# Streaming weights in transfers of 1024 columns through four places instead of 2048 columns through two, in a decoder-layer kernel

## The chip, the cores and the metric

The kernel runs on one core of a Trainium2 chip. The metric is the time of one execution on the device in microseconds (us). The core has engines that run their own instruction lists side by side and wait for each other on semaphores: PE (TensorE, the matmuls, with PEld for its weight loads), ACT (ScalarE), DVE (VectorE), POOL (GpSimd) and SP (SyncE, which here only issues transfers). Data come from the device memory by DMA.

## What is computed

One decoder layer on 512 tokens of width 1024, in float32:

```python
f = swiglu(rms_norm(h, ffn1_norm_pre[l]), ffn1_w_gate[l], ffn1_w_up[l], ffn1_w_down[l])
h = h + 0.5 * rms_norm(f, ffn1_norm_post[l])
u = rms_norm(h, mix_norm_pre[l])
proj = u @ w_in[l]
q, k, v, xr, yr, gl = jnp.split(proj, splits, axis=-1)
...
attn_d = attn.astype(x.dtype).reshape(B, S, ATTN_OUT_WIDTH) @ w_attn_branch[l]
...
rec_d = rec @ w_rec_branch[l]
gates = jax.nn.sigmoid(gl).reshape(B, S, N_BRANCHES, D_MODEL)
merged = gates[:, :, 0] * attn_d + gates[:, :, 1] * rec_d
h = h + rms_norm(merged @ w_out[l], mix_norm_post[l])
f = swiglu(rms_norm(h, ffn2_norm_pre[l]), ffn2_w_gate[l], ffn2_w_up[l], ffn2_w_down[l])
h = h + 0.5 * rms_norm(f, ffn2_norm_post[l])
```

with `swiglu(x) = (silu(x @ w_gate) * (x @ w_up)) @ w_down`, a hidden width of 2816, twelve heads of dilated window attention, and a gated linear recurrence (RG-LRU) as the second branch. Nearly all of the data that are read are weights, and each weight is used once.

## The kernel before, in words

**Products.** Each float32 operand is split into a high part and the rest (`split`, L294: ACT copies the high part at L295, then DVE subtracts at L296), and a product is three matmuls: high with high, high with rest, rest with high. Where two matrices are multiplied with the same input, or a product can be cut in four quarters, seven products of half size stand for eight (`seven`, L738; `seven_on`, L709; `seventh`, L699, with the matmuls at L705 to L707). For these, sums of the weights' quarters are needed; `w_forms` (L661) makes them on DVE (L668 to L670 and L673) and then splits four results `a`, `b`, `c` and `d` on ACT and DVE. `w_forms_within` (L681) does the same in another order.

**The two feed-forward parts** (`ffn`, L772) go through 22 hidden blocks of 128. The first few (6 in the first part, 3 in the second) are plain products (`std`). Each later block `f` has one weight block `gu` of 2048 columns (gate and up side by side), whose forms are made one block ahead (`prep`), and one product of seven (`prod`). Hidden blocks come in parts of four; the products with the down matrix of a finished part are put beside the next blocks in four steps (`prepd` with `d_forms`, L883, and `down7`, L947, matmuls at L956 to L958). These steps take 2, 1, 2 and 1 weight blocks of 1024 columns. `merge` (L967) adds up the quarters after the last part. Between the two feed-forward parts stand the mixer's stages: values, queries and keys (double blocks named `pair`), attention, recurrence, output.

**The stream.** All weights lie in device memory in the order of use. `stream_plan` (L103) lists the blocks with their widths; `stream_groups` (L159) packs consecutive blocks into groups of at most `RAW_W` = 2048 columns, and a group is one transfer of up to 1024 KB (128 partitions of 8 KB). `raw_of` (L232) hands out the next block of the list; with the first block of a group it takes a place of the tag `raw` (two places, L238) and issues the transfer on SP (L240). A place can be written again when all readers of what it held are done. A double block (`gu`, `pair`, and `vq`, four of them for the values, two of which go straight to buffers of their own) fills one place. Two blocks of 1024 share one if they follow each other and neither is cut off by a double block. A single block of 1024 between two double blocks has a whole place to itself.

**Order.** The kernel is written as one program, and `tc.high_priority(offset=...)` moves instructions ahead: the fetching and forming of weights by `AHEAD` = 100, the taking of results out of the accumulators by `EVAC` = 200. From the priorities, the dependences and the expected readiness of data, a fixed order of instructions for each engine comes out when the program is built. At run time an engine goes through its list in that order and waits where an operand is not there. SP issues the stream's transfers in the order of use.

**The start.** `fetch_start` (L270) loads eight blocks of 512 columns into two places by eight transfers, each beside a piece of the input.

Of the kernel before, what the change touches and what calls it, by code (L numbers as in the profile page):

```python
# [10 lines left out]
F32 = mybir.dt.float32  # L11
# [5 lines left out]
P = 128  # L17
T = 512
D = 1024
# [9 lines left out]
NH = 4  # L29
EPS = 1e-6  # L30
HB = 256
RAW_W = 2048
NEG = -1.0e30

FIRST_ON = {1: 5, 2: 5}
# [67 lines left out]
def stream_plan():  # L103

    plan = []

    def down(n, a, half):
        for kk in range(part_blocks(a)):
            plan.append((("down", n, a, half, kk), 1024))

    def ffn(n):
        for ev in ffn_order(n):
            if ev[0] == "std":
                plan.append((("gate", n, ev[1]), 1024))
                plan.append((("up", n, ev[1]), 1024))
            elif ev[0] == "prep":
                plan.append((("gu", n, ev[1]), 2048))
            elif ev[0] == "prepd":
                for q in SEVEN_RAW[ev[2]]:
                    plan.append((("dq", n, ev[1], q), 1024))  # L120
        for half in range(2):
            down(n, len(FF_PARTS) - 1, half)

    def qk(h):
        for g in range(NG):
            plan.append((("pair", g * 4 + h, 12 + g * 4 + h), 2048))

    ffn(1)
    del plan[:4]
    for k in range(KC):  # L130
        plan.insert(k, (("start", k), 512))
    for k in range(4):
        plan.append((("v", 0, k), 1024))
    for q in ("g0", "g1", "u0", "u1"):
        plan.append((("vq", q), 2048))
    for h in range(NH):
        qk(h)
    for c in range(0, KC, 2):
        plan.append((("pair", 52 + c, 53 + c), 2048))
    for m in range(0, KC, 2):  # L140
        plan.append((("attn", m), 1024))
    for what, h in LRU_ORDER:
        if what == "gates":
            plan.append((("lru", h), 1024))
        elif (what, h) in PAIRED:
            plan.append((pair_key(what, h), 2048))
        else:
            for c in GATE1[h] if what == "gate1" else (2 * h, 2 * h + 1):
                plan.append((("in", COLUMN[what] + c), 1024))
    for m in range(KC):  # L150
        plan.append((("rec", m), 1024))
    for half in range(2):
        for kk in range(4):
            plan.append((("out", half, kk), 1024))
    ffn(2)
    return plan


def stream_groups():  # L159
# [22 lines left out]
def hybrid_layer(ctx: ExitStack, tc: tile.TileContext, xT: bass.AP, xN: bass.AP, wst: bass.AP,  # L182
                 first: bass.AP, rows: bass.AP, consts: bass.AP, bias: bass.AP, out: bass.AP):
    nc = tc.nc
    DVE, ACT, PE = nc.vector, nc.scalar, nc.tensor
# [3 lines left out]
    wpool = ctx.enter_context(tc.tile_pool(name="wpool", bufs=4))  # L189
# [42 lines left out]
    def raw_of(key, dst=None):  # L232

        g, i = state["g"], state["i"]
        grp = groups[g]
        if i == 0:
            w = grp[-1][1] + grp[-1][2]
            raw = dst if dst is not None else wpool.tile([P, RAW_W], F32, name="raw", tag="raw", bufs=2)  # L238
            src = bass.AP(tensor=wst.tensor, offset=wst.offset + state["off"], ap=[[w, P], [1, w]])
            nc.sync.dma_start(raw[:, :w], src)  # L240
            state["raw"] = raw
            state["off"] += w * P
        k, o, w = grp[i]
        assert k == key, (k, key)
        src = state["raw"][:, o:o + w]
        if i + 1 == len(grp):
            state["g"], state["i"] = g + 1, 0
        else:
            state["i"] = i + 1
        return src  # L250

    def fetch(key, slot=None, ahead=0):

# [15 lines left out]

    def fetch_start():  # L270

        raws = [wpool.tile([P, RAW_W], F32, name="raw", tag="raw", bufs=2) for _ in range(2)]
        wts = []
        for k in range(KC):
            raw = raws[k // 4][:, (k % 4) * 512:(k % 4) * 512 + 512]
            if k == 0:
                raw = first_t[:, :512]
                nc.sync.dma_start(hm(k), xT[k])
                nc.sync.dma_start(raw, first[:, :512])
            else:  # L280
                nc.sync.dma_start(raw, bass.AP(tensor=wst.tensor, offset=wst.offset + (k - 1) * 512 * P,
                                               ap=[[512, P], [1, 512]]))
                nc.sync.dma_start(hm(k), xT[k])
            if k % 2 == 0:
                wt = w8()
            o = (k % 2) * 512
            wts.append((wt[:, 0, o:o + 512], wt[:, 1, o:o + 512], raw))
        state["g"], state["off"] = KC, (KC - 1) * 512 * P
        return wts
# [4 lines left out]
    def split(dh, dl, src):  # L294
        ACT.activation(dh, src, AF.Copy)  # L295
        DVE.tensor_sub(dl, src, dh.bitcast(F32))  # L296
# [364 lines left out]
    def w_forms(key):  # L661

        with tc.high_priority(offset=AHEAD):
            raw = raw_of(key)
            u0, u1, g0, g1 = (raw[:, i * 512:(i + 1) * 512] for i in range(4))
            s12 = spool[0].tile([P, 2, 512], F32, name="s12", tag="s", bufs=2)
            s1, s2 = s12[:, 0, :], s12[:, 1, :]
            DVE.tensor_add(s2, u0, u1)  # L668
            DVE.tensor_add(s1, s2, g0)
            DVE.tensor_add(u0, u0, g0)  # L670
            a, b, c, d = w8(), w8(), w8(), w4()
            split(a[:, 0, :], a[:, 1, :], raw[:, 1024:2048])
            DVE.tensor_add(g1, s1, g1)  # L673
            split(b[:, 0, :], b[:, 1, :], s12.rearrange("p s c -> p (s c)"))
            split(c[:, 0, :], c[:, 1, :], raw[:, 0:1024])
            split(d[:, 0, :], d[:, 1, :], g1)
            lo, hi = slice(0, 512), slice(512, 1024)
            return {"p1": a[:, :, lo], "p2": a[:, :, hi], "p6": b[:, :, lo], "p5": b[:, :, hi],
                    "p7": c[:, :, lo], "p4": c[:, :, hi], "p3": d}

    def w_forms_within(key):  # L681

        with tc.high_priority(offset=AHEAD):
            raw = raw_of(key)
            u0, u1, g0, g1 = (raw[:, i * 512:(i + 1) * 512] for i in range(4))
            lo, hi = slice(0, 512), slice(512, 1024)
            d, a, c, b = w4(), w8(), w8(), w8()
            split(d[:, 0, :], d[:, 1, :], u1)
            split(a[:, 0, :], a[:, 1, :], raw[:, 1024:2048])
            DVE.tensor_add(u1, u0, u1)  # L690
            DVE.tensor_add(u0, u0, g0)
            DVE.tensor_add(g0, u1, g0)
            split(c[:, 0, :], c[:, 1, :], raw[:, 0:1024])
            DVE.tensor_add(g1, g0, g1)
            split(b[:, 0, :], b[:, 1, :], raw[:, 1024:2048])
            return {"p1": a[:, :, lo], "p2": a[:, :, hi], "p7": c[:, :, lo], "p5": c[:, :, hi],
                    "p6": b[:, :, lo], "p3": b[:, :, hi], "p4": d}

# [327 lines left out]
    u1 = act_of(*act_two(ap1))  # L1026
# [10 lines left out]
    for k in range(KC):  # L1037
        wh, wl, raw = wts[k]
# [48 lines left out]
    with ExitStack() as mx:  # L1087
# [38 lines left out]
        def values_two(steps, then):  # L1126


            def v_of(g):
                return apool.tile([P, 4, T], F32, name="vals", tag=f"v{g}")  # L1130

            def flat(v):
                return v.rearrange("p k t -> p (k t)")

            def add(dst, x, y):
                with tc.high_priority(offset=AHEAD):
                    for h in range(2):
                        cs = slice(h * D, h * D + D)
                        DVE.tensor_add(dst[:, cs], x[:, cs], y[:, cs])

            def form(src):
                with tc.high_priority(offset=AHEAD):
                    ws = [w8(), w8()]
                    for h, w in enumerate(ws):
                        split(w[:, 0, :], w[:, 1, :], src[:, h * D:h * D + D])
                return ws

            def prod(p, w, pss, start):
# [11 lines left out]
                        ACT.activation(dst, ps, AF.Copy, scale=scale)  # L1160

            with tc.high_priority(offset=AHEAD):
                g0, g1 = raw_of(("vq", "g0")), raw_of(("vq", "g1"))
                u0 = raw_of(("vq", "u0"), flat(v_of(1)))
                u1 = raw_of(("vq", "u1"), flat(v_of(2)))
            sd = flat(both[:, 4:8, :])
            b, y, z = [aux_ps(), aux_ps()], [acc_ps(), acc_ps()], [aux_ps(), acc_ps()]
            c5, c6 = ([facc[:, i + j, :] for j in range(2)] for i in (0, 2))
# [192 lines left out]
        for c in range(0, KC, 2):  # L1361
            g, u = tmp("g"), tmp("u")
# [12 lines left out]
    with ExitStack() as mx:  # L1375
# [20 lines left out]
        o, w = SMALL["ap"]  # L1396
# [210 lines left out]
    grow5, _ = gains(ap2, 4)  # L1607
# [58 lines left out]

def _block(key, a):
    kind = key[0]
    if kind in ("gate", "up"):
        return _cols(a[f"ffn{key[1]}_w_{kind}"], key[2] * P)  # L1670
    if kind in ("down", "out"):
        if kind == "out":
            w, r0, half = a["w_out"], key[2] * 2 * P, key[1]
        else:
            w, r0, half = a[f"ffn{key[1]}_w_down"], (FF_PARTS[key[2]][0] + key[4] * 2) * P, key[3]
# [18 lines left out]
    if kind == "start":  # L1694
        k = key[1]
# [47 lines left out]
```

## Time and profile before

| what | value |
|---|---|
| median of 3 runs | 1215.67 us (1215.48 to 1216.31) |
| the profiled execution | 1217.76 us |
| its span, first to last instruction | 1215.9 us |
| what lies around the span | 1217.76 - 1215.9 = 1.9 us |
| mean granted TensorE clock | 0.998 of full |
| read from device memory | 138.06 MB, 119 GB/s with what is written |
| transfers issued on SP at L240 | 107 of 1024 KB and 18 of 512 KB, and 2 of 1024 KB to `vals` |

The profile is that of one execution. Busy time of PE is the union of its matmuls as the profiler models them; matmuls overlap, so a matmul of 128x256 that is recorded with 0.28 us follows the one before it at 0.12 us when nothing holds it up. The chain of waits goes back from the last instruction to what released each one, and in it every matmul has only the time to the next. The table of waits lists, for each engine, how long it stood idle and what ended that; a wait in the middle of an engine's list holds all that is behind it.

### The profile page before, as it was taken

How to read it: one execution, taken by the hardware profiler on the slowest of the kernel's cores; microseconds unless marked ns; L12 is line 12 of the kernel's file. 1: busy time of each engine (PE TensorE's matmuls, PEld its weight loads, DVE VectorE, ACT ScalarE, POOL GpSimd, SP SyncE). 2: the span in 40 equal slices, each digit the busy share in tenths (PEclk: the TensorE clock that was granted, in tenths of full speed). 3: DMA queues.
4: the chain of work that ended last, by engine and by line, in shares of the span. 5: the costliest groups of instructions: out<-in, count | busy, mean ns of one | idle time of the engine just before them, and what ended most of it. 6: DMA issues, size and time to landing. Idle time of an engine off the chain costs nothing.

```text
span 1215.9 us, 19433 instructions
## 1 busy us (share of the span) xinstructions
PE 1204.9 (99%) x7754; PEld 1100.9 (91%) x7754; DVE 1011.2 (83%) x1536; ACT 813.1 (67%) x1391; POOL 26.2 (2%) x51
## 2 busy tenths in 40 slices
PE   9999999999999999999999999999999999999998
PEld 8889999989888999999989888888899999999996
DVE  7999888889689887888766899875798888889964
ACT  7567777777656664665736888934566677878763
POOL 0000000000002000000000000000100000000000
PEclk9999999999999999999999999999999999999999
DMA  6223333334535122222222342224443333333341
GB/s 248 104 87 122 122 121 122 122 121 156 224 126 178 70 81 103 79 82 101 76 99 87 139 160 83 105 104 173 149 148 121 122 122 121 122 122 121 139 174 70
DMA packets 30123, 149.80 MB, mean 123 GB/s; under 512 B 3408, under 2 KB 6864, under 8 KB 16080
## 3 DMA queue, kind: packets, MB, share of 16 engines
q1 hardware_dynamic: 22464, 131.08, 30.2%
q0 software_dynamic: 7280, 17.30, 4.2%
q8 instruction: 61, 1.00, 0.3%
q14 instruction: 30, 0.25, 0.1%
q10 hardware_dynamic: 288, 0.17, 0.0%
HBM read 138.06 MB, written 6.29 MB: 119 GB/s over the span
## 4 chain that ended last, share of the span: by engine, by line
PE 94%; DVE 3%; ACT 2%; DMA 1%; issue 1%; DVEq 0%; ACTq 0%
PE acc L705 15%; PE acc L706 15%; PE acc L707 15%; PE acc L308 7%; PE acc L310 7%; PE acc L309 7%; PE aux L956 4%; PE aux L957 4%; PE aux L958 4%; PE acc L426 2%; PE acc L424 2%; PE acc L425 2%; PE aux L425 1%; PE aux L424 1%; PE aux L426 1%; ACT w L295 1%
## 5 line engine op out<-in xcount | busy, mean ns | idle before, releaser
L705 PE MATMUL acc<-big,w 128*128 128x256 f32 x1240 | 352.0, 284 | 1.9 <-ACT acc L719 1.9
L706 PE MATMUL acc<-big,w 128*128 128x256 f32 x1240 | 351.9, 284 | 0.0
L707 PE MATMUL acc<-big,w 128*128 128x256 f32 x1240 | 351.6, 284 | 0.0
L296 DVE TENSOR_TENSOR w<-raw,w 128x1024 fp32r<-128x1024 f32 (+1 forms) x272 | 297.4, 1099 | 64.7 <-ACT w L295 59.5
L295 ACT ACTIVATE w<-raw 128x1024 fp32r<-128x1024 f32 (+1 forms) x272 | 259.4, 959 | 101.7 <-PE acc L310 39.4
L705 PEld LDWEIGHTS acc<-big,w 128*128 128x128 f32 x1240 | 237.7, 192 | 4.2 <-ACT acc L719 2.1
L706 PEld LDWEIGHTS acc<-big,w 128*128 128x128 f32 x1240 | 237.8, 192 | 1.9
L707 PEld LDWEIGHTS acc<-big,w 128*128 128x128 f32 x1240 | 237.8, 192 | 0.0
L956 PE MATMUL aux<-w,xf 128*128 128x512 f32 x224 | 87.6, 396 | 1.0 <-ACT w L295 1.0
L957 PE MATMUL aux<-w,xf 128*128 128x512 f32 x224 | 88.0, 393 | 0.0
L958 PE MATMUL aux<-w,xf 128*128 128x512 f32 x224 | 87.7, 392 | 0.0
L295 ACT ACTIVATE w<-s 128x1024 fp32r<-128x1024 f32 x51 | 54.0, 1060 | 21.1 <-PE acc L707 13.6
L296 DVE TENSOR_TENSOR w<-s,w 128x1024 fp32r<-128x1024 f32 x51 | 62.2, 1219 | 1.0 <-ACT w L295 0.9
L668 DVE TENSOR_TENSOR s<-raw 128x512 f32<-128x512 f32 x51 | 35.1, 688 | 29.0 <-DMA raw<-in_w 29.0
L308 PE MATMUL acc<-xf,w 128*128 128x512 f32 (+1 forms) x168 | 59.0, 353 | 0.0
L309 PE MATMUL acc<-xf,w 128*128 128x512 f32 (+1 forms) x168 | 58.7, 350 | 0.0
L310 PE MATMUL acc<-xf,w 128*128 128x512 f32 (+1 forms) x168 | 58.5, 349 | 0.0
L719 ACT ACTIVATE c<-acc 128x256 f32<-128x256 f32 x74 | 28.3, 383 | 36.0 <-PE acc L707 35.8
L956 PEld LDWEIGHTS aux<-w,xf 128*128 128x128 f32 x224 | 42.1, 190 | 9.8 <-ACT w L295 2.0
L958 PEld LDWEIGHTS aux<-w,xf 128*128 128x128 f32 x224 | 42.4, 189 | 8.9
L308 PE MATMUL acc<-big,w 128*128 128x512 f32 x128 | 49.8, 389 | 0.0
L309 PE MATMUL acc<-big,w 128*128 128x512 f32 x128 | 49.8, 389 | 0.0
(436 smaller groups left out, 2757.9 us busy)
## 6 DMA issues: line engine op xcount, KB each, us to landing
raw<-in_w SPq DMA_DIRECT2D x107, 1024.0 KB, 4.8
raw<-in_w SPq DMA_DIRECT2D x18, 512.0 KB, 3.5
big<-xf POOLq DMA_DIRECT2D x6, 512.0 KB, 3.3
gains<-in_rows POOLq DMA_DIRECT2D x5, 512.0 KB, 4.2
h<-in_x SPq DMA_DIRECT2D x8, 256.0 KB, 5.2
h<-in_xn POOLq DMA_DIRECT2D x4, 512.0 KB, 6.9
kept_m<-h POOLq DMA_DIRECT2D x4, 512.0 KB, 2.9
vals<-in_w SPq DMA_DIRECT2D x2, 1024.0 KB, 7.0
```

The source lines that it names most:

```text
L295: ACT.activation(dh, src, AF.Copy)
L296: DVE.tensor_sub(dl, src, dh.bitcast(F32))
L308: PE.matmul(ps, wh, xh, start=first, stop=False)
L309: PE.matmul(ps, wh, xl, start=False, stop=False)
L310: PE.matmul(ps, wl, xh, start=False, stop=last)
L424: PE.matmul(ps, x.hi[k][:, bl], wh, start=k == 0 and not seeded, stop=False, skip_group_check=True)
L705: PE.matmul(ps, wh, xh, start=start and k == 0, stop=False, skip_group_check=True)
L706: PE.matmul(ps, wh, xl, start=False, stop=False, skip_group_check=True)
L707: PE.matmul(ps, wl, xh, start=False, stop=k == 3, skip_group_check=True)
L956: PE.matmul(ps, xh, wh, start=first and j == 0, stop=False, skip_group_check=True)
L957: PE.matmul(ps, xh, wl, start=False, stop=False, skip_group_check=True)
L958: PE.matmul(ps, xl, wh, start=False, stop=j == 1, skip_group_check=True)
```

## The change

`RAW_W` goes from 2048 to 1024, and the tag `raw` has four places of 1024 columns instead of two of 2048, in the same memory. `stream_plan` turns every block of 2048 columns into two of 1024 with the keys `lo` and `hi`, so that no group has more than one block of 1024 columns and every transfer of the stream has 512 KB. `raw_two` takes the two halves; `w_forms`, `w_forms_within` and `values_two` take their quarters from two tiles instead of one. The sums and splits are the same in number and size.

```diff
-RAW_W = 2048
+RAW_W = 1024
...
-    return plan
+
+    return [(key + (i,), RAW_W) if width > RAW_W else (key, width)
+            for key, width in plan for i in (("lo", "hi") if width > RAW_W else ("",))]
...
-            raw = dst if dst is not None else wpool.tile([P, RAW_W], F32, name="raw", tag="raw", bufs=2)
+            raw = dst if dst is not None else wpool.tile([P, RAW_W], F32, name="raw", tag="raw", bufs=4)
...
+    def raw_two(key, dst=None):
+
+        return [raw_of(key + (n,), None if dst is None else dst[:, i * RAW_W:(i + 1) * RAW_W])
+                for i, n in enumerate(("lo", "hi"))]
+
...
-        raws = [wpool.tile([P, RAW_W], F32, name="raw", tag="raw", bufs=2) for _ in range(2)]
+        raws = [wpool.tile([P, RAW_W], F32, name="raw", tag="raw", bufs=4) for _ in range(4)]
...
-            raw = raws[k // 4][:, (k % 4) * 512:(k % 4) * 512 + 512]
+            raw = raws[k // 2][:, (k % 2) * 512:(k % 2) * 512 + 512]
...
     def w_forms(key):
 
         with tc.high_priority(offset=AHEAD):
-            raw = raw_of(key)
-            u0, u1, g0, g1 = (raw[:, i * 512:(i + 1) * 512] for i in range(4))
+            ur, gr = raw_two(key)
+            u0, u1, g0, g1 = (r[:, i * 512:(i + 1) * 512] for r in (ur, gr) for i in range(2))
...
             a, b, c, d = w8(), w8(), w8(), w4()
-            split(a[:, 0, :], a[:, 1, :], raw[:, 1024:2048])
+            split(a[:, 0, :], a[:, 1, :], gr)
             DVE.tensor_add(g1, s1, g1)
             split(b[:, 0, :], b[:, 1, :], s12.rearrange("p s c -> p (s c)"))
-            split(c[:, 0, :], c[:, 1, :], raw[:, 0:1024])
+            split(c[:, 0, :], c[:, 1, :], ur)
             split(d[:, 0, :], d[:, 1, :], g1)
...
             with tc.high_priority(offset=AHEAD):
-                g0, g1 = raw_of(("vq", "g0")), raw_of(("vq", "g1"))
-                u0 = raw_of(("vq", "u0"), flat(v_of(1)))
-                u1 = raw_of(("vq", "u1"), flat(v_of(2)))
+                g0, g1 = raw_two(("vq", "g0")), raw_two(("vq", "g1"))
+                u0, u1 = flat(v_of(1)), flat(v_of(2))
+                for q, u in (("u0", u0), ("u1", u1)):
+                    raw_two(("vq", q), u)
```

More of the change, by code (lines that the diff above doesn't have):

```diff
@@ L683, in w_forms_within @@
         with tc.high_priority(offset=AHEAD):
-            raw = raw_of(key)
-            u0, u1, g0, g1 = (raw[:, i * 512:(i + 1) * 512] for i in range(4))
+            ur, gr = raw_two(key)
+            u0, u1, g0, g1 = (r[:, i * 512:(i + 1) * 512] for r in (ur, gr) for i in range(2))
             lo, hi = slice(0, 512), slice(512, 1024)
@@ L688, in w_forms_within @@
             split(d[:, 0, :], d[:, 1, :], u1)
-            split(a[:, 0, :], a[:, 1, :], raw[:, 1024:2048])
+            split(a[:, 0, :], a[:, 1, :], gr)
             DVE.tensor_add(u1, u0, u1)
@@ L692, in w_forms_within @@
             DVE.tensor_add(g0, u1, g0)
-            split(c[:, 0, :], c[:, 1, :], raw[:, 0:1024])
+            split(c[:, 0, :], c[:, 1, :], ur)
             DVE.tensor_add(g1, g0, g1)
-            split(b[:, 0, :], b[:, 1, :], raw[:, 1024:2048])
+            split(b[:, 0, :], b[:, 1, :], gr)
             return {"p1": a[:, :, lo], "p2": a[:, :, hi], "p7": c[:, :, lo], "p5": c[:, :, hi],
@@ L1133, in flat, with two_of @@
                 return v.rearrange("p k t -> p (k t)")
+            def two_of(a):
+                return a if isinstance(a, list) else (a[:, :D], a[:, D:])
             def add(dst, x, y):
                 with tc.high_priority(offset=AHEAD):
-                    for h in range(2):
-                        cs = slice(h * D, h * D + D)
-                        DVE.tensor_add(dst[:, cs], x[:, cs], y[:, cs])
+                    for d, x_, y_ in zip(*(two_of(a) for a in (dst, x, y))):
+                        DVE.tensor_add(d, x_, y_)
             def form(src):
@@ L1143, in form @@
                     ws = [w8(), w8()]
-                    for h, w in enumerate(ws):
-                        split(w[:, 0, :], w[:, 1, :], src[:, h * D:h * D + D])
+                    for w, half in zip(ws, two_of(src)):
+                        split(w[:, 0, :], w[:, 1, :], half)
                 return ws
@@ L1668, in _block @@
     kind = key[0]
+    if key[-1] in ("lo", "hi"):
+        i = ("lo", "hi").index(key[-1])
+        return _block(key[:-1], a).reshape(P, 2, RAW_W)[:, i]
     if kind in ("gate", "up"):
```

## The prediction, made before the result was known

> **What bounds the kernel now.** I begin with the page's busy times, then take what PE itself waited for.
>
> ```profile
> PE 1204.9 (99%) x7754; PEld 1100.9 (91%) x7754; DVE 1011.2 (83%) x1536; ACT 813.1 (67%) x1391; POOL 26.2 (2%) x51
> ```
>
> ```profile
> PE acc L705 <- ACT acc L719: 1.9, 1, 1.9
> PE aux L1033 <- DVE eps L226: 1.1, 1, 1.1
> PE aux L956 <- ACT w L295: 1.0, 5, 0.2
> PE aux L1154 <- DVE w L296: 0.3, 1, 0.3
> ```
>
> PE is busy for 99% of the span, so the change can win only where PE stands still or runs slowly, and these rows (engine, what it waited for, total us, times, longest) are nearly all of that. One wait of 1.9 us is the largest. The wait at L1033 is the program's start, which the change leaves alone. So I look for the 1.9 us in time, by busy time in three stretches of 16 us.
>
> ```profile
> 242.00:258.00 16.00, 16.00 (x114) 15.04 (x113) 14.29 (x20) 13.60 (x24) 0.00 (x0) 1.00 0.30 98
> 258.00:274.00 16.00, 14.13 (x93) 13.09 (x93) 11.23 (x15) 9.51 (x17) 0.00 (x0) 0.89 0.39 132
> 274.00:290.00 16.00, 16.00 (x114) 15.02 (x113) 14.74 (x20) 12.41 (x22) 0.00 (x0) 1.00 0.26 99
> ```
>
> The columns are PE, PEld, DVE, ACT and POOL busy, the granted clock and two of DMA. In the middle stretch PE is busy 14.13 of 16.00 us, and the clock is 0.89 where its neighbours have 1.00. The chain of waits there says why.
>
> ```profile
> 257.78 1.15 DVE w L296
> 258.95 7.32 DMA raw<-in_w
> 266.35 1.06 ACT w L295
> 267.40 0.27 ACT g L877
> 267.68 0.28 ACT acc L719
> 268.00 0.38 PE acc L705
> ...
> 270.04 0.43 PE aux L956
> ```
>
> DVE finished the last split of the double block of hidden block 18, that freed the place, and the transfer of block 19 started and took 7.32 us. ACT stood before the split of its gate half (L295). Behind that in ACT's list were the SiLU of block 18 (L877) and the copy out of an accumulator (L719), which need nothing from that transfer, and PE needs the copy. ACT's timeline has the length of the block:
>
> ```profile
> 266.35 1.06 ACT L295 ACTIVATE w<-raw 128x1024 fp32r<-128x1024 f32 x1 [3.16 <-DMA raw<-in_w]
> ```
>
> The same transfer is usually faster, by the page's list of transfers and that of the stretch before:
>
> ```profile
> raw<-in_w SPq DMA_DIRECT2D x107, 1024.0 KB, 4.8
> raw<-in_w SPq DMA_DIRECT2D x18, 512.0 KB, 3.5
> ```
>
> ```profile
> raw<-in_w SPq DMA_DIRECT2D x1, 1024.0 KB, 7.3
> ```
>
> (The second fence is the answer for 258.5 to 260 us.) So block 19 came 7.3 - 4.8 = 2.5 us late. Elsewhere the forms wait for data too, on DVE (L668) and on ACT (L295), without PE losing:
>
> ```profile
> DVE s L668 <- DMA raw<-in_w: 29.0, 21, 3.1
> ACT w L295 <- DMA raw<-in_w: 13.4, 16, 3.5
> ```
>
> The change therefore acts on a chain (place free, transfer, forms) that is close behind PE in the feed-forward parts, and in one place ahead of it.
>
> **The change part by part.** *More transfers.* 59 double blocks become 118 transfers and the 50 remaining pairs of single blocks become 100; with the 18 single ones that is 236 instead of 127, 109 more. SP issues them:
>
> ```profile
> L240 SPq DMA_DIRECT2D raw<-in_w x125: 327/328/331, 11.3 to 1174.2; - x125
> ```
>
> 109 x 0.33 = 36 us more on SP, whose list holds nothing else but a few loads and the output, and which mostly waits for places to come free (the row of its waits):
>
> ```profile
> SPq L240 <- DVE w L296: 731.8, 96, 22.4
> ```
>
> I cost it at nothing: 36 us lie within 731.8 us of waiting. If both halves start together, the second starts 0.33 us later, which the transfer of the first covers, as it needs 3.5 us. DVE and ACT get one wait more for each double block and no work.
>
> *A half lands earlier.* From 512 KB to 1024 KB the time goes from 3.5 to 4.8 us: 1.3 us for 512 KB, and 2.2 us that don't depend on the size. If a second transfer paid these 2.2 us after the first, the second half would land at 7.0 us. If the 2.2 us overlap, it lands at 4.8 us plus at most 0.33. The nearest rows are those of the next transfer, the second for the stretch of 260.5 to 261.5 us:
>
> ```profile
> 260.93 0.33 SPq L240 DMA_DIRECT2D raw<-in_w  x1
> ```
>
> ```profile
> raw<-in_w SPq DMA_DIRECT2D x1, 1024.0 KB, 7.8
> ```
>
> It landed at 260.93 + 7.8 = 268.7, the one before at 258.95 + 7.3 = 266.3: 2.4 us apart for a whole 1024 KB, less than its 2 x 1.3 of data time. The fixed part overlaps, so I take 4.8 to 5.1 us for both halves. [...]
>
> *Places come free in halves.* The columns of a double block are read last at different times. For block 18, `d` (from the second half) and `c` (from the first) end as follows, and the down blocks of the step before (L899 reads both, the split at 245.09 only `g0`) like this:
>
> ```profile
> 237.37 1.22 DVE L899 TENSOR_TENSOR sum<-raw 128x1024 f32<-128x1024 f32 x1
> ...
> 245.09 1.23 DVE L296 TENSOR_TENSOR w<-raw,w 128x1024 fp32r<-128x1024 f32 x1 [0.51 <-ACT w L295]
> ...
> 255.29 0.69 DVE L296 TENSOR_TENSOR w<-raw,w 128x512 fp32r<-128x512 f32 x1
> ...
> 257.70 1.22 DVE L296 TENSOR_TENSOR w<-raw,w 128x1024 fp32r<-128x1024 f32 x1
> ```
>
> The four places go round: 18 lo, 18 hi, then `u1` of the down blocks in the place of `g0` (free at 246.3), then 19 lo in the place of `u0`, free since 238.6. So 19 lo starts right behind `u1`, near 246.7 instead of 258.95. 19 hi needs the place of 18 lo and starts at 258.95 as before, with half the bytes. Two of every four hidden blocks are like this (after a step with a single down block); in the other two both halves start together and only the first lands earlier. All forms but the first sum need the second half, so what counts is 1.3 us on half of the blocks.
>
> *What that is worth at 258.* If 19 hi is as much slowed as the whole was, it lands 1.3 us earlier, at 265.0; if it takes the usual 3.5 us, at 262.45, before ACT, which became free at 266.35 - 3.16 = 263.19, asks for it. PE loses 16.00 - 14.13 = 1.87 us there now; with 1.3 us of it saved 0.57 remain, with all, nothing. Take 1.6. The clock costs as much again: at 0.89 over 14.13 us of work it is 0.11 x 14.13 = 1.55 us, and the row at 270.04 has 0.43 us for a matmul that elsewhere has 0.24 (below). This fell behind an idle time of 1.87 us; behind the short waits at L956 it didn't. So it goes with the stall, and I take the 1.55 whole. [...]
>
> *The other waits.* The five at L956 look like this one:
>
> ```profile
> 223.03 0.12 PE acc L707
> 223.15 0.23 PE aux L956
> ...
> 225.67 0.24 PE aux L958
> 225.91 0.02 issue
> 225.94 0.60 ACT ea L961
> 226.54 0.95 ACT w L295
> 227.49 0.04 issue
> 227.53 0.73 PE aux L956 x2
> ```
>
> ACT copies an accumulator (L961) and only then splits the weight that PE wants next; no transfer is in the chain. From 225.91 PE has 12 matmuls of the next product at 0.12 us (the row at 223.03), to 227.35; it begins L956 at 227.53 and needs 0.73 us for two matmuls of 0.23: 0.18 + 0.27 = 0.45 us lost. The order of ACT's list decides, so I take no gain, with bounds of plus and minus 5 x 0.45 = 2.3 us.
>
> *Start, values, tail.* In the start the first stream transfer waits behind the start's own on SP; the wait at L1154 ends on DVE work, not on data; the last transfer lands long before the end. Nothing for each.
>
> *Sum.* 1.6 + 1.55 = 3.15 us, say 3.2. The profiled execution has 1217.76 us (1215.9 of span and 1.9 around it): 1217.76 - 3.2 = 1214.6. The runs' median of 1215.67 is 2.1 us below that execution; taken off, **1212.5 us** (-0.26%).
>
> **The rivals.** *(a) No change.* Only here does PE lose to a late transfer, and the 2.1 us between profile and median is near what the stall costs. If the timed runs don't have it, there is nothing to win: 1215.67 less a few tenths, 1215.4. It also comes so if the change doesn't do what it says: where the last split of the first half sets the start, no transfer moves. For it: SP waits mostly for DVE's splits. Against: the list of waits has 21 + 16 = 37 waits for data.
>
> *(b) Slower, by ACT's order.* The order of the lists is made anew from an earlier readiness of data. If forms are put further ahead, ACT stands before a half that isn't there while accumulators wait behind it, which is the chain of 258 in small. The price is that of the small stalls, 0.45 us, in those of the 35 `gu` blocks (16 and 19) whose halves start together, about 18: 8.1 us; -3.2 + 8.1 = +4.9, 1220.6. It decides from 3.2 / 0.45, 7 such blocks, on. For it: DVE and ACT already wait for data 37 times, so the lists are made with data in mind that come too late. Against: no half comes later than its whole did.
>
> *(c) Slower, by the fixed part.* If the 2.2 us are paid one after another, the second half comes 2.2 us later than now. At 258 ACT's 3.16 us cost PE 1.87, so 1.29 are covered; 0.9 us x 35 = 32 us less 3.2: 1244. [...]
>
> *(d) Faster still.* The lists come out better and the five small stalls go too: 1212.5 - 2.3 = 1210.2.
>
> **How the numbers follow.** The forecast with (d) has 0.42 (0.34 and 0.08), (a) 0.27, (b) 0.27, (c) 0.04. A measurement of this kernel can tell about 0.2% from no change, which is 2.4 us; the forecast lies only just beyond. Faster by more than that is the forecast and (d), the same is (a), slower (b) and (c). The range goes from 1209.8, under (d), to 1223, which holds the middle of (b) and leaves out (c) and the worse part of (b).
>
> **What would show it.** Right: the list of transfers has 232 `raw` of 512 KB near 3.5 us; the transfer of 19 lo is issued near 247; the stretch 258 to 274 has PE at 16.00 and a clock of 1.00; L705 no longer waits for L719. Rival (a): the same, but the time stays. (b): more waits of PE on ACT, and longer waits of ACT's L295 for `raw`. (c): transfers of 512 KB with landings near 5.7 us where two start together. It is wrong altogether if the order of ACT or DVE at L295, L719 and L961 differs so much that stalls turn up in stages which have none now.

## The result and the profile after

Over 22 runs of each kernel the median went from 1216.43 us (1213.97 to 1220.45) to 1218.91 us (1216.41 to 1222.43). The ratio is **1.0022, with a 95% interval of 1.0013 to 1.0031: slower by 0.22%**, where 0.26% faster was forecast. The profiled execution of the changed kernel has 1216.87 us and a span of 1215.1 us. It is 2.0 us below its own median, and the profiled one of before lay 1.3 us above its median, so the two spans, 1215.9 and 1215.1, must not be subtracted. The places in the traces count, and the time comes from the runs.

The line numbers move by 7: the split is now L302 (ACT) and L303 (DVE), the matmuls of the sevens L712 to L714, the copy out of an accumulator L726, those of `down7` L963 to L965, and a stream transfer is issued at L242.

The page of the changed kernel, busy times and the stream's transfers:

```profile
PE 1202.6 (99%) x7754; PEld 1099.5 (90%) x7754; DVE 1009.6 (83%) x1536; ACT 816.2 (67%) x1393; POOL 26.1 (2%) x51
...
raw<-in_w SPq DMA_DIRECT2D x232, 512.0 KB, 3.5
```

The transfers are as forecast. The stretch of block 19, in the same columns as before:

```profile
258.00:274.00 16.00, 16.00 (x115) 15.04 (x114) 12.66 (x17) 12.45 (x23) 0.00 (x0) 1.00 0.40 134
```

PE is busy throughout and the clock is 1.00: the stall that the change was forecast to remove is gone. But the list of PE's waits (total us, times, longest) looks like this:

```profile
PE acc L712 <- ACT acc L726: 2.6, 1, 2.6
PE aux L315 <- ACT w L302: 1.5, 1, 1.5
PE aux L1040 <- DVE eps L228: 1.1, 1, 1.1
PE aux L963 <- ACT w L302: 0.7, 3, 0.3
```

The first row has the same pair of lines as the 1.9 us of before, and it is another stall. The chain of waits shows where it is:

```profile
302.56 6.88 DMA raw<-in_w
...
309.47 1.06 ACT act L302
310.52 0.28 ACT acc L726
...
310.85 0.39 PE acc L712
```

It stands at 310 us, at the end of the first feed-forward part. A half with a block of the down matrix took 6.88 us instead of 3.5, ACT stood before its split (into the slot `act`), and the copy that PE needed was behind that in ACT's list. ACT's timeline has the rows:

```profile
306.39 0.37 ACT L884 ACTIVATE g<-acc 128x256 f32<-128x256 f32 x1
309.47 1.06 ACT L302 ACTIVATE act<-raw 128x1024 fp32r<-128x1024 f32 x1 [2.71 <-DMA raw<-in_w]
310.43 0.37 ACT L726 ACTIVATE acc<-acc 128x256 f32<-128x256 f32 x1
```

The second row of the waits is at 690 us, in the recurrence, and has no transfer in its chain:

```profile
686.98 0.60 DVE gt L1538
687.59 0.67 DVE sig L1466
...
688.28 0.02 ACT rec L302
688.31 0.51 issue
688.82 1.05 ACT w L302
...
689.91 0.73 PE aux L315 x2
```

DVE had other work of the recurrence (L1538) ahead of the last sum of `sig` (L1466), ACT waited for that sum with the split of `rec`, and the weight that PE needed was split only after it.

Both are questions of order. Instruction by instruction, the two kernels have the same work on PE, ACT and DVE, but when the program is built other lists come out: 347 of ACT's 1273 places hold another instruction than before, 899 of DVE's 1536, and 758 of PE's 7626 (by the lists as they are written out for the runs below; the page counts some more records of ACT and PE). That gives the theory that I tested: **the transfers and places win what was forecast, and the new order of the lists loses more, most of it at these two places.** The rivals are that the transfers themselves cost time, and that the order costs a little everywhere.

### The profile page after: what moved, and what is told of

Read it like the earlier page. It is cut to its first block, busy times and chain, and to the rows that moved or that the text cites. A ratio compares the mean times of both kernels' runs of the same rounds, so it can differ in the third digit from the quotient of the medians.

```text
span 1215.1 us, 19769 instructions
## 1 busy us (share of the span) xinstructions
PE 1202.6 (99%) x7754; PEld 1099.5 (90%) x7754; DVE 1009.6 (83%) x1536; ACT 816.2 (67%) x1393; POOL 26.1 (2%) x51
## 4 chain that ended last, share of the span: by engine, by line
PE 94%; DVE 2%; ACT 1%; DMA 1%; issue 0%; DVEq 0%; ACTq 0%
PE acc L712 14%; PE acc L713 14%; PE acc L714 14%; PE acc L315 7%; PE acc L317 7%; PE acc L316 7%; PE aux L963 4%; PE aux L964 4%; PE aux L965 4%; PE acc L432 2%; PE acc L431 2%; PE acc L433 2%; DMA raw<-in_w 1%; PE aux L433 1%; PE aux L431 1%; PE aux L432 1%
## 5 line engine op out<-in xcount | busy, mean ns | idle before, releaser
L712 PE MATMUL acc<-big,w 128*128 128x256 f32 x1240 | 351.7, 284 | 2.6 <-ACT acc L726 2.6
L714 PE MATMUL acc<-big,w 128*128 128x256 f32 x1240 | 351.8, 284 | 0.0
L303 DVE TENSOR_TENSOR w<-raw,w 128x1024 fp32r<-128x1024 f32 (+1 forms) x272 | 297.7, 1098 | 45.4 <-ACT w L302 39.7
L302 ACT ACTIVATE w<-raw 128x1024 fp32r<-128x1024 f32 (+1 forms) x272 | 259.7, 958 | 99.1 <-PE acc L317 45.1
L712 PEld LDWEIGHTS acc<-big,w 128*128 128x128 f32 x1240 | 237.6, 192 | 4.7 <-ACT acc L726 2.8
L714 PEld LDWEIGHTS acc<-big,w 128*128 128x128 f32 x1240 | 237.7, 192 | 0.0
L963 PE MATMUL aux<-w,xf 128*128 128x512 f32 x224 | 87.3, 392 | 0.7 <-ACT w L302 0.7
L965 PE MATMUL aux<-w,xf 128*128 128x512 f32 x224 | 87.2, 389 | 0.0
L303 DVE TENSOR_TENSOR w<-s,w 128x1024 fp32r<-128x1024 f32 x51 | 62.2, 1219 | 3.7 <-ACT w L302 3.5
L302 ACT ACTIVATE w<-s 128x1024 fp32r<-128x1024 f32 x51 | 54.0, 1058 | 12.7 <-PE acc L714 9.2
L726 ACT ACTIVATE c<-acc 128x256 f32<-128x256 f32 x74 | 28.2, 382 | 40.7 <-PE acc L714 40.6
L963 PEld LDWEIGHTS aux<-w,xf 128*128 128x128 f32 x224 | 41.9, 188 | 9.1 <-ACT w L302 1.3
L965 PEld LDWEIGHTS aux<-w,xf 128*128 128x128 f32 x224 | 42.1, 188 | 8.8
L315 PE MATMUL acc<-big,w 128*128 128x512 f32 x128 | 49.8, 389 | 0.0
L316 PE MATMUL acc<-big,w 128*128 128x512 f32 x128 | 49.8, 389 | 0.0
L317 PE MATMUL acc<-big,w 128*128 128x512 f32 x128 | 49.8, 389 | 0.0
```

What stands on the lines that cost most here:

```text
L315: PE.matmul(ps, wh, xh, start=first, stop=False)
L316: PE.matmul(ps, wh, xl, start=False, stop=False)
L317: PE.matmul(ps, wl, xh, start=False, stop=last)
L712: PE.matmul(ps, wh, xh, start=start and k == 0, stop=False, skip_group_check=True)
L714: PE.matmul(ps, wl, xh, start=False, stop=k == 3, skip_group_check=True)
L963: PE.matmul(ps, xh, wh, start=first and j == 0, stop=False, skip_group_check=True)
```

## The experiments

All ratios are to the kernel before, run on the same chip alongside, with 95% intervals. e1 and e2 ran on one chip, e3 to e6 on a second, e7 and e8 on a third, so a difference within one of these sets is surer than one between two of them.

| run | what it is | median us | ratio |
|---|---|---|---|
| the change | | 1218.91 | 1.0022 [1.0013, 1.0031] |
| e1 | the change, before's lists | 1213.54 | 0.9980 [0.9971, 0.9989] |
| e2 | before's places and lists, halves as transfers | 1215.21 | 0.9995 [0.9986, 1.0005] |
| e3 | the change, its own lists written out | 1219.27 | 1.0026 [1.0016, 1.0035] |
| e4 | e3, before's order at 294 to 316 us | 1214.89 | 0.9996 [0.9987, 1.0005] |
| e5 | e4, before's order at 641 to 725 us too | 1213.87 | 0.9983 [0.9974, 0.9992] |
| e6 | e1, the change's order at 294 to 316 us | 1220.77 | 1.0041 [1.0028, 1.0053] |
| e7 | e3, the loads of `h` at 301 us cut to 1/8 (the residual of the other columns is left out) | 1215.93 | 1.0004 [0.9994, 1.0014] |
| e8 | the change's order to 294 us, before's from there | 1212.09 | 0.9971 [0.9962, 0.9980] |

**The transfers without the new order (e1).** The order of the three lists is written out and kept by dependences that need no semaphore:

```diff
         hybrid_layer(tc, *args)
+        keep_order(tc)
...
+def keep_order(tc):
+    want = json.loads(zlib.decompress(base64.b85decode(ORDER)))
...
+        for a, b in zip(want[e], want[e][1:]):
+            tc.add_manual_dep(ins[b], ins[a].name, mybir.DependencyInfo(
+                mybir.DependencyClass.NoSync, mybir.DependencyReason.DATA), reason="order")
```

> The changed kernel (four places of 1024 columns, 236 transfers), with the instructions of PE, ACT and DVE held in the exact order that they have in the kernel before. Theory A (order: the 2.5 us come from the new order of the lists, the transfers themselves win a little): ratio to before 0.998 to 1.000, so 0 to 2.5 us faster than before. Theory B (transfers: twice as many transfers are late more often, or cost their waits on DVE and ACT; the order does not matter): ratio near 1.002, 2.5 us slower, as the changed kernel.

The ratio is 0.9980: faster by 0.2%, 2.4 us, beside the 3.2 us of the forecast. PE's wait for L726 isn't in the list of waits any more:

```profile
PE aux L1040 <- DVE eps L228: 1.1, 1, 1.1
PE aux L963 <- ACT w L302: 1.0, 5, 0.2
PE aux L1163 <- DVE w L303: 0.3, 1, 0.3
```

The order alone makes 1.0022 / 0.9980 = 1.0042, or 5.1 us.

**Twice the transfers without the places (e2).** Before's two places of 2048 columns and before's lists, but each transfer of 1024 KB issued as two:

```diff
-            src = bass.AP(tensor=wst.tensor, offset=wst.offset + state["off"], ap=[[w, P], [1, w]])
-            nc.sync.dma_start(raw[:, :w], src)
+            h = min(w, 1024)
+            for o in range(0, w, h):
+                src = bass.AP(tensor=wst.tensor, offset=wst.offset + state["off"] + o * P, ap=[[h, P], [1, h]])
+                nc.sync.dma_start(raw[:, o:o + h], src)
```

> The kernel before with its two places of 2048 columns and its order of instructions held, but each 1024 KB transfer issued as two of 512 KB, one behind the other, into the same place. Only the number and size of the transfers changes. Theory A: ratio 0.999 to 1.001. Theory B: ratio near 1.002. If the first experiment is faster than before and this one is not, what wins is that places come free in halves.

The ratio is 0.9995, with 1 in its interval. Twice the transfers, together with what they save at block 19, cost nothing that can be measured; the further 0.0015 of e1, on the same chip, point to the four places. What is left of block 19's stall is in its waits, 0.5 us (at L707 here) where the kernel before had 1.9:

```profile
PE acc L707 <- ACT acc L721: 0.5, 1, 0.5
```

**Both kernels once more.** One profile more of each, unchanged, to see whether the stalls belong to the kernels:

> The kernel before once more, for a second profile. Both theories: PE loses only little in most places; if the stall of block 19 near 258 us is a rare event, it is not there this time and the span is near 1213 us; if it is fixed, PE again waits 1.9 us for the copy behind the split of block 19.

> The changed kernel once more, for a second profile, since its first profiled execution (1216.87 us) lies 2 us under its median. Theory A: waits of PE on ACT or DVE that stand at the same places as in the first profile (near 310 and 690 us), 2 us or more together. Theory B: PE loses at other places than in the first profile, each time behind a transfer that needs over 5 us.

They do: before again loses PE time at 267 us (16.00 - 14.29 = 1.7 us), and the changed kernel stands until 310.9 and 691.5 us, within 2 us of the places of the first profile. The clock is another matter, below.

**The order written out as it is (e3).** A control: if writing an order out were what gained, this would gain too.

> The kernel after the change with the order of its PE, ACT and DVE lists written out as it has it anyway: a control for the writing out. If the order of the lists is what costs (theory), nothing changes: ratio to the kernel before 1.0022 as measured, within 1.001 and 1.003, with the stalls of 2.7 us at 310 us and 1.7 us at 690 us in place. If the gain of the run with before's order came from writing an order out as such (rival), this run has the gain too: ratio 0.998.

The ratio is 1.0026, so it isn't.

**One place undone (e4).** The lists are those of e3 but for 22 places of ACT's and 17 of DVE's, which hold the same instructions in both orders; in short (`order` stands for a kernel's written-out lists):

```diff
-want = order(after)
+want = order(after); want[ACT][356:378] = order(before)[ACT][356:378]
+want[DVE][359:376] = order(before)[DVE][359:376]
```

> The kernel after the change in its own order, but 22 places of ACT's list and 17 of DVE's (294 to 316 us) in the order of before. Theory (the cost sits in two places, here and at 690 us): the stall of 2.7 to 3.05 us at 310 us goes, 0.23%, and the ratio to before falls from 1.0022 to 0.9998; the stall at 690 us stays. If the clock lost behind the stall (1.8 us more in one of two profiles) goes too, 0.9985. Rival (the cost is spread over the hundred places where the lists differ): the stall goes from the profile but the ratio stays at 1.0015 or above. The transfers at 302 to 308 us should still take near 7 us in either case, since they share the time with the loads of POOL.

The ratio falls from 1.0026 to 0.9996, by 0.0030 or 3.6 us; 0.0024 was forecast for the stall alone and 0.0037 with the clock. The wait at 690 us stays (1.7 us). The half still takes 7.0 us, by the answer for its issue, so what has gone is what stood behind it:

```profile
raw<-in_w SPq DMA_DIRECT2D x1, 512.0 KB, 7.0
```

ACT's timeline of e1, which has the same order here, shows how: the copy comes first, and the splits of the two late blocks stand behind it.

```profile
308.92 0.37 ACT L726 ACTIVATE acc<-acc 128x256 f32<-128x256 f32 x1
...
314.42 1.06 ACT L302 ACTIVATE tx<-raw 128x1024 fp32r<-128x1024 f32 x1 [1.38 <-DMA raw<-in_w]
315.39 1.04 ACT L302 ACTIVATE act<-raw 128x1024 fp32r<-128x1024 f32 x1
```

**The second place undone as well (e5).** The edit is that of e4, with 71 places of ACT's list, 77 of DVE's and 239 of PE's between 641 and 725 us:

> As the run before it, and the stretch of 641 to 725 us also in the order of before on PE, ACT and DVE. Theory: the stall of 1.66 us at 690 us goes as well, 0.14% less than the run with 300 us alone: ratio 0.9985, within 0.1% of the 0.998 with all of before's order; what is left are the three short waits of the last feed-forward part, 0.7 us or 0.06%. Rival (spread): 1.001 or above. If undoing 690 only lets a stall turn up elsewhere, as high as the run with 300 us alone.

The ratio falls by another 0.0013 (1.6 us) to 0.9983, within 0.0003 of e1. The intervals of e4 and e5 overlap, so the second place's share is less sure than the first's. In the chain of waits the split of the weight now stands ahead of that of `rec`, right behind the matmul that frees its place:

```profile
684.68 0.24 PE acc L317
...
684.95 1.06 ACT w L302
686.01 0.53 ACT rec L302
```

So two stretches of the lists, 106 us together, hold 0.9983 to 1.0026 = 0.43% of the 0.46% between e1 and e3. A third place is left in: the last of PE's waits at L963, near 1080 us, is 0.2 us with before's lists, 0.3 us in the changed kernel and 1.4 us in this profile.

**The first place alone (e6).** The reverse of e4: e1 with the change's order at 294 to 316 us.

> The reverse: before's order everywhere (ratio 0.998 so far), with after's order only in the 22 places of ACT's list and 17 of DVE's at 294 to 316 us. Theory: the stall of PE on an accumulator's copy at 310 us is back with 2.6 to 3.1 us, and the ratio is 0.998 + 0.0023 = 1.0003, more by up to 0.0015 if the clock falls behind it. Rival (spread): 0.998 to 0.9985. If the stall needs the earlier order too (when the transfers before it were issued), no stall here and 0.998.

The ratio is 1.0041, 0.0061 (7.4 us) above e1, and more than forecast. Transfer and stall are both larger in this combination (7.63 us, and 3.5 us in the list of waits), and the clock is 0.96 from 300 to 316 us and 0.97 from there to 350. The chain of waits:

```profile
305.69 7.63 DMA raw<-in_w
...
313.34 1.06 ACT act L302
314.40 0.28 ACT acc L726
...
314.72 0.58 PE acc L712
```

In the same stretch a smaller wait appeared that neither order has by itself (L963 waiting for an ACT copy, 1.0 us). The direction is shown; the size is that of this combination.

**The cause of the slow transfer (e7).** At 301 us POOL starts to load `h` for the mixer. The lists are those of e3, but the loads are short:

```diff
     for b in range(4):
-        nc.gpsimd.dma_start(hb(b), xN[b])
+        nc.gpsimd.memset(hb(b)[:, 128:], 0.0)
+        nc.gpsimd.dma_start(hb(b)[:, :128], xN[b][:, :128])
```

> The kernel after the change with its own order written out, but the four loads of h from in_xn at 301 to 304 us bring 128 of 1024 columns, and POOL sets the other columns to zero (so the residual that is added back is left out for them). Theory (the half that ACT waits for at 310 us is slowed by those loads, which share the 16 DMA engines with it): the transfer issued at 302.6 us takes 3.5 to 4.4 us instead of 6.9, lands before ACT is free at 306.8 us, the stall of 2.7 us goes though no list is changed, and the ratio falls from 1.0026 by 0.0022 to 0.0030, to 0.9996 to 1.0004. Rival (the halves slow one another, four in flight on one queue): the transfer still takes 6 us or more, and the ratio stays at 1.002 to 1.003. The stall at 690 us stays in both.

The ratio falls from 1.0026 to 1.0004, without any change of the lists; 0.9996 to 1.0004 was forecast, and the wait at 690 us stays (2.0 us). The transfers issued beside each other are, in the changed kernel (answer for 302.4 to 302.7 us) and in e7 (302.6 to 303 us):

```profile
h<-in_xn POOLq DMA_DIRECT2D x1, 512.0 KB, 5.4
raw<-in_w SPq DMA_DIRECT2D x1, 512.0 KB, 6.9
```

```profile
raw<-in_w SPq DMA_DIRECT2D x1, 512.0 KB, 3.4
h<-in_xn POOLq DMA_DIRECT2D x1, 64.0 KB, 2.1
```

And ACT, which waited 2.71 us there, goes through without waiting:

```profile
306.79 0.36 ACT L884 ACTIVATE g<-acc 128x256 f32<-128x256 f32 x1
307.05 1.05 ACT L302 ACTIVATE act<-raw 128x1024 fp32r<-128x1024 f32 x1
308.00 0.38 ACT L726 ACTIVATE acc<-acc 128x256 f32<-128x256 f32 x1
```

So the stall at 310 us needs both: the loads that slow the half, and the order in which the copy stands behind it. Taking away either one takes it away.

**The better order of each stretch (e8).** Up to 294 us the change's order has none of the small stalls at L963 (e1 has three there), and from 294 us on before's is better:

> Transfers and places of the change; the lists in after's order up to 294 us, where that order has no small stalls, and in before's order from there on, where it has neither the stall at 310 nor the one at 690 us. Theory (stalls at places make up the difference): the three stalls of about 0.36 us at 89, 167 and 227 us of the run with all of before's order go, 1.3 us less than its 1213.5: 1212.2, ratio 0.9970 (0.998 less 0.0011). Rival (each place of the lists has its own noise, and what is saved early is lost again in the stages behind): as that run, 0.998, or up to 0.999.

The ratio is 0.9971, 1212.09 us: faster than both kernels, by 0.3% and 0.5%, with the same transfers and the same work. It is 1.1 us under e1 by the two ratios, but their intervals overlap and the chips differ, so the gain over e1 isn't shown by the times. Its waits for ACT at L963 are down from five to two:

```profile
PE aux L1040 <- DVE eps L228: 1.1, 1, 1.1
PE aux L963 <- ACT w L302: 0.4, 2, 0.2
PE aux L1163 <- DVE w L303: 0.3, 1, 0.3
```

## Why the prediction was wrong

**More transfers: right.** 232 halves of 512 KB with 3.5 us stand in the page, and with the places and lists of before, twice the transfers give 0.9995.

**A half lands earlier, and the fixed parts overlap: right.** In the changed kernel, the two transfers issued together at 235.19 us, the second 0.60 us after the first, took 3.4 and 4.0 us, so both were there 4.6 us after the first was issued; 4.8 to 5.1 was forecast. In e1, the two issued at 286.38 us, again 0.60 us apart, took a median of 4.1 us. The 2.2 us that don't depend on the size are the prediction's estimate from the 3.5 and 4.8 us of before's page; paid one after another, they would have made it 7.0 us.

**Places come free in halves: right for the first half, wrong for the second.** With before's lists, by which the prediction reckons, 19 lo is issued at 246.37 us (e1), and 246.7 was forecast. 19 hi was to need the place of 18 lo and to start at 258.95. It is issued at 256.04, right when the split of `d` ends (255.32 + 0.69 = 256.01), and `d` is read from 18 hi. DVE's and SP's timelines of e1:

```profile
255.32 0.69 DVE L303 TENSOR_TENSOR w<-raw,w 128x512 fp32r<-128x512 f32 x1
```

```profile
256.04 0.33 SPq L242 DMA_DIRECT2D raw<-in_w  x1
```

In the changed kernel, with its own lists, both halves go out earlier still:

```profile
244.55 0.33 SPq L242 DMA_DIRECT2D raw<-in_w  x1
```

```profile
250.80 0.33 SPq L242 DMA_DIRECT2D raw<-in_w  x1
```

**What that is worth at 258: near in the sum, in part by luck.** 3.2 us were forecast, and e1 gains 2.4 us in all (1.3 to 3.5 by its interval); no run shows how much of that falls here. The stall comes again in before's second profile, with 1.71 us, and in e1 all of it is gone and not 1.6 us: the second half goes out 2.9 us earlier than forecast, and with the 3.5 us of the page would be there at 259.5, an estimate. The 1.55 us for the clock don't come again. So one term was too small and the other not sure, and that their sum lies in e1's interval is partly luck. Before's second profile, without any change, has the stall and a full clock (the column behind POOL):

```profile
258.00:274.00 16.00, 14.29 (x100) 13.25 (x99) 11.38 (x16) 10.63 (x19) 0.00 (x0) 1.00 0.38 132
```

So the clock fell behind this stall in one of two profiled executions, the one in which it was longer (1.87 us).

**The other waits: the step that failed.** "The order of ACT's list decides, so I take no gain, with bounds of plus and minus 5 x 0.45 = 2.3 us". It counted what the five waits already there could do, and not that new lists can put a wait where there is none. The end of the first feed-forward part and the recurrence, where those waits came, stand in no term of the sum. The order's term was +5.1 us (from e3 over e1, 1.0046, it is 5.6), more than twice the bound and larger than the gain: -2.4 + 5.1 = +2.7 us, the measured 0.22%. Undoing the two places gave 3.6 + 1.6 = 5.2 us. In the changed kernel's profile the two waits are 2.6 + 1.5 = 4.1 us; the granted clock, 0.9981 on average over its 22 runs and 0.9989 over the 11 of e1, would make 0.0008 x 1215 = 1.0 us more, an estimate that no run tests.

**Rival (b) was right in kind and wrong in place and price.** It had ACT standing before a half that isn't there while accumulators wait behind it, and that is the chain at 310 us. But it priced this as 0.45 us in each of 18 `gu` blocks, from the small stalls, and had 8.1 us; it came once, in a down block, for 2.6 us. The reason given against it, that "no half comes later than its whole did", is true of this half and says nothing of order: the half that ACT waits for goes out at 302.56 us, while before it shared a transfer issued some 9 us later, by SP's timeline of the kernel before, whose first of two issues this is:

```profile
312.08 2.99 SPq L240 DMA_DIRECT2D raw<-in_w  x2
```

Its split was moved ahead of a copy that had been safely in front. That the earlier expected readiness of the data moved it follows from how the lists are made; no run tested this step by itself. The 690 us stall is of another kind, with no transfer in it, and no rival had it; the prediction's last sentence, on stalls "in stages which have none now", is the case that came.

**The price stood in a row of before; the place did not.** The row is this: the two transfers of 1024 KB issued behind POOL's loads, at 312 and 315 us, took a median of 8.1 us instead of 4.8:

```profile
raw<-in_w SPq DMA_DIRECT2D x2, 1024.0 KB, 8.1
```

That cost PE nothing, since ACT's copies for PE stood ahead of their splits, so the prediction gave it no price. The row alone would not have told the place, though: three other transfers of 1024 KB in the same profile, issued at 831.1, 833.4 and 873.9 us, took 8.3, 8.3 and 9.1 us, and in the changed kernel PE doesn't wait from 825 to 885 us.

## What to carry to other kernels

Where the lists are made anew with every build, a change of transfers or buffers is two changes: measure it once with the old order held, and once as it comes, before judging it; here these gave 0.9980 and 1.0022. To price a new order blind, don't take the small stalls that are there: look for the slowest transfers that cost nothing today, find what stands right behind their readers in the list, and take the full lateness for each (here 8.1 - 4.8 = 3.3 us, for stalls of 2.6 us in the changed kernel and 3.5 in e6). That would not have found the wait at 690 us, which has no transfer in its chain. And when the order decides, stretches of two good orders can be put together, which gave 0.9971.

## What the runs showed of the hardware

**The half beside POOL's loads took twice as long, and at first POOL's queue had nearly all of the DMA engines.** The 232 halves of the changed kernel have a median of 3.5 us, and the one issued beside POOL's loads at 302.56 us took 6.9 us; in e7, with those loads cut from 512 to 64 KB each, it took 3.4 us. In the changed kernel, the shares of the 16 DMA engines by queue (number of packets, MB, share) are, from 303 to 306 us and from 306 to 309.4 us:

```profile
q0 software_dynamic: 254, 0.96, 94.1%
q1 hardware_dynamic: 5, 0.02, 2.1%
```

```profile
q0 software_dynamic: 225, 0.82, 59.5%
q1 hardware_dynamic: 153, 0.56, 41.8%
```

Together they have 96.2% and 101.3%. In the first stretch POOL's queue (q0, which from 300 to 316 us moved 2.10 MB, the four loads of 512 KB) has 94.1%, though the half is issued at 302.56; in the second both move, with 59.5% and 41.8%. Why the stream's queue (q1) had only 2.1% in the first, no run here shows.

**The granted clock was lower beside a stall of 1.7 us at one place, and not beside one of 2.6 us at another.** The changed kernel's stall of 2.6 us at 310 us left the clock at 1.00; its repetition, with a stall of 2.9 us (PE busy for 13.11 us of 16), had 0.89. At 690 us the 1.5 us of the change left 1.00, and the longer wait of e4, 1.7 us, had 0.86 (windows of the changed kernel, of its repetition and of e4; the clock is the third number from the end):

```profile
300.00:316.00 16.00, 13.42 (x97) 12.61 (x97) 9.61 (x12) 9.84 (x15) 2.10 (x4) 1.00 0.92 333
...
680.00:692.00 12.00, 10.50 (x57) 8.85 (x56) 10.39 (x14) 9.31 (x14) 0.00 (x0) 1.00 0.30 89
```

```profile
300.00:316.00 16.00, 13.11 (x88) 12.40 (x88) 9.08 (x12) 9.35 (x15) 2.10 (x4) 0.89 0.90 328
```

```profile
680.00:692.00 12.00, 10.26 (x54) 9.04 (x53) 11.97 (x18) 7.79 (x13) 0.58 (x2) 0.86 0.28 89
```

So in these executions the length of a stall doesn't tell by itself whether the clock falls: 1.7 us had 0.86 at 690 us, and 2.6 us had 1.00 at 310 us. At each of the two places the longer of the two stalls has the lower clock, as at 258 us; these few executions are no rule, and what decides it no run here shows. By the prediction's estimate for block 19, 1.87 us of stall and 1.55 us of clock, that stall cost nearly twice its length.
